# Gate and up projections of a feed-forward block by Strassen's seven products instead of eight

## The chip, the cores and the metric

One Trainium2 chip, one of its cores. The metric is the device time of one execution in microseconds (us). The kernel before has a median of 674.45 us over three runs (674.44 to 675.98).

## What is computed

One transformer block on 512 tokens of 1024 features in float32: an input norm, eight latent heads and eight sparse heads, an output projection, and a gated feed-forward part with `D_FF` = 2816. The change lies in the feed-forward part, the last lines of the reference:

```python
h = h + mixed @ w_out[l]
f = rmsnorm(h, norm_ffn_g[l])
h = h + (jax.nn.silu(f @ w_gate[l]) * (f @ w_up[l])) @ w_down[l]
return rmsnorm(h, final_norm_g)
```

## The kernel before, in words

Every float32 product is made of three products in the tensor engine's narrower `fp32r` format. Each operand is split into a rounded high part and the exact rest, and `mm3` (L167 to 170) issues high times high (L168), one part's rest times the other's high part (L169, L170), all three summing in one bank of PSUM:

```python
def mm3(o, lh, ll, rh, rl, start, stop):
    pe.matmul(o, lh, rh, start=start, stop=False)
    pe.matmul(o, lh, rl, start=False, stop=False)
    pe.matmul(o, ll, rh, start=False, stop=stop)
```

The first operand is stationary (128 x 128, loaded by an LDWEIGHTS that the profile counts under PEld), the second streams through as 128 rows by up to 512 columns.

**Order.** Up to the first two feed-forward tiles a planner (`Plan`, L55) puts the jobs of PE, DVE, ACT and POOL into a fixed order when the program is built: it knows an estimated time for each job, the jobs it waits for, the buffers it takes and frees and a priority. Each engine then runs its own list strictly in that order. The order never changes at run time, so an instruction that waits holds up everything behind it on its engine. Loads are issued from SP in the planned order too. From the third feed-forward tile on the order before is that of the code.

**Around the change.** The second half of the output projection (L1324 to 1338) makes eight products of twelve matmuls, named `mm<-w_hi,omh` in the profile, with the token tile `t` in the outer loop and the column half `nh` in the inner one; `add_out` (L1305, DVE) adds each to the residual `h`. `norm_turned` (L307) then takes a token tile: squares on ACT or DVE (L321, L323), the root of their mean on POOL (L327 to 330), scaling on DVE (L333, `xn`), eight transposes on PE (L348, `tp<-ident,xn`), a rounded copy on ACT (L362, `fTh`) and the exact rest on DVE (L368, `fTl`). So four token tiles need 32 transposes.

**Gate and up.** 22 tiles of 128 feed-forward columns. For each, two weight units of 128 x 1024 (gate, up) come in by DMA, are rounded on ACT (L158, `w_hi`) and subtracted on DVE (L162, `w_lo`); a ring of four units runs ahead. The first two tiles are made in two halves of 256 tokens (L1365, streams of 256 columns, banks `sc` and `pv`), so that they can start before the last token tiles are turned. The other twenty use streams of 512 tokens: 2 units x 8 feature tiles x 3 = 48 matmuls a tile, into the banks `mm` and `sc` in turn. `activated` (L1389) makes `silu(gate) * up` (ACT, then DVE L1403) and splits it into `a`.

**Down.** For each of the 22 tiles the weight unit `w_down` is split and 24 matmuls of 512 columns go into eight banks that hold the whole output (4 token tiles x 2 halves). The last four tiles are taken token tile by token tile, so that each one's final norm and output run beside the next one's products.

Of the kernel before, what the change touches and what calls it, by code (L numbers as in the profile page):

```python
# [10 lines left out]
F32 = mybir.dt.float32  # L11
# [18 lines left out]
# column ranges of w_in  # L30
# [7 lines left out]
def row_bcast(ap, n):  # L38
    """A DRAM row of n numbers, read into all partitions."""
    return bass.AP(tensor=ap.tensor, offset=ap.offset, ap=[[0, P], [1, n]])  # L40


class Job:
# [4 lines left out]
    def seen(self, e):  # L48
        """when an engine can go on after it"""
        if self.lag is not None:  # L50
            return self.end + self.lag
        return self.end + Plan.LAGS.get((self.eng, e), 0 if self.eng in (e, None) else Plan.LAG)


class Plan:  # L55
    """Puts jobs into the order in which their engines come to them: a job is a piece of one engine's work with
    its estimated time, the jobs it waits for, the buffers it takes and leaves, and its priority."""
# [9 lines left out]
    def add(self, ways, fn=None, after=(), pri=0.0, takes=(), frees=(), lag=None):  # L67
        """ways: (engine, ns), or several of them with the function that does it there"""
# [6 lines left out]
    def pe_end(self, t, ns, busy):  # L75
        """when the tensor engine is through with ns of work at its full clock: it has half of that after an idle tick"""
# [45 lines left out]
# priorities of the projections, as places in the row of softmaxes  # L122
# [6 lines left out]
def block_kernel(ctx: ExitStack, tc: tile.TileContext, I, out):  # L129
# [25 lines left out]
    def split(hi, lo, src, scale=None, lo_eng=None):  # L155
        """hi: src (times scale) rounded to the product's width; lo: the exact rest."""
# [10 lines left out]
    def mm3(o, lh, ll, rh, rl, start, stop):  # L167
        pe.matmul(o, lh, rh, start=start, stop=False)  # L168
        pe.matmul(o, lh, rl, start=False, stop=False)  # L169
        pe.matmul(o, ll, rh, start=False, stop=stop)  # L170
# [8 lines left out]
    class Weights:  # L179
        """Units of weights (at most 4 KB a partition), in the order of their use: loaded as they are,  # L180
        then split into two parts; loads run ahead of the splits and those ahead of the products."""
# [25 lines left out]
        def get(self, u, ahead=None):  # L207
            """unit u; the slots that its predecessors leave are filled"""
# [14 lines left out]
    kpe = px.tile([96, S], F32, name="kpe")      # rotary part of the latent keys, in rows 64-95  # L223
# [9 lines left out]
    kc = kqv.tile([P, 2, 2, 32], F32R, name="kc")    # compressed keys: group, high and low  # L233
# [4 lines left out]
    # ================= projections of the normalised input =================  # L238
# [12 lines left out]
    # weights of the latent projections: two feature tiles a unit  # L251
# [18 lines left out]
    plan = Plan(mm=2, sc=2, tp=2, pv=2, raw=2, part=3, s=4, pt=0, of=1, tmp=1, sq=1, bn=2, s4=2, rr=1, q=2, raw2=2, part2=4, cn=2, xn=2)  # L270
# [24 lines left out]
    def swapped(dst, src, sn, lead):  # L295
        """dst = the halves of src exchanged, times sn."""
# [61 lines left out]
    def split_parts(parts, after, pri, frees):  # L358
        """parts: (high, low, source, scale, columns) of one bank; all its first readers come before the second ones"""
# [21 lines left out]
    def copied(dst, src, n, after, pri, psum=True, scale=None, takes=(), frees=()):  # L381
        """a copy by the engine that comes to it first"""
# [6 lines left out]
    def split_pieces(h, l, raw, n, after, pri, takes=(), frees=()):  # L389
        """a split of operands in SBUF, given as functions, on the engines that come to it first"""  # L390
# [5 lines left out]
    def weight(pl, srcs, shape, pri, raw, part, nraw, npart, after=(), pieces=2, parts=None):  # L396
        """loads a unit of weights and splits it along its first axis, piece by piece"""
# [1136 lines left out]
```

## Time and profile before

| what | value |
|---|---|
| median of three runs | 674.45 us |
| profiled execution, as the page gives it (its span) | 670.7 us |
| median above the span | 3.75 us |
| PE busy | 643.0 us (96%) |
| DVE, ACT, POOL busy | 365.8, 284.6, 157.5 us |
| first feed-forward matmul starts | 299.20 us |
| down projection starts | 542.38 us |
| last matmul starts | 661.85 us |

The page states the profiled execution by its span alone, from the first to the last instruction, so the median stands 3.75 us above it; no other time of that execution is given. Times below are counted from the start of the span. In a row of the profile, "x160" is a count, the two numbers after the bar are the busy time in us and the mean of one in ns, and "idle before" is how long the engine had stood still. Matmuls overlap in the array, so a matmul's own length (392 ns) is not its cost; the distance from one start to the next is. In a table of stretches each engine has its busy time and, in brackets, its instructions that touch the stretch; then come the granted clock of the tensor engine (1.00 is full), the DMA share and GB/s.

### The profile page before, as it was taken

Reading aid. Unit: us, or ns where it says so; the run is one execution under the profiler, and the core shown is the slowest. Engines: PE = TensorE matmul, PEld = TensorE weight load, DVE = VectorE, ACT = ScalarE, POOL = GpSimd, SP = SyncE. Lnnn points to the kernel's source line nnn. Section 1 sums busy time; section 2 is a strip of 40 time slices with the busy share of each in tenths; the row PEclk is TensorE's granted clock in tenths of the full one; section 3 lists DMA queues with packets and bytes.
Section 4 is the critical chain, followed back from the end, with each engine's and each line's share of the span. In section 5 each row is a group of like instructions: output and inputs, shape, how many; then the busy total and the mean of one; then the engine's idle time right before and its main releaser. Section 6 shows DMA issues by size and latency. Waiting matters only on the chain.

```text
span 670.7 us, 9389 instructions
## 1 busy us (share of the span) xinstructions
PE 643.0 (96%) x3311; PEld 539.9 (80%) x3311; DVE 365.8 (55%) x867; ACT 284.6 (42%) x646; POOL 157.5 (23%) x234
## 2 busy tenths in 40 slices
PE   5899899999999999999999999999999999999994
PEld 3877698888987788789888888888888888888883
DVE  5956777898999988783343333333242422222234
ACT  4532236888997985233232222323232322221123
POOL 4621345347774742550000000000000000000013
PEclk9999889998999999999999999999999999999998
DMA  8437530121004211432232324242424243222202
GB/s 269 128 53 136 151 94 1 33 79 33 1 5 167 94 55 64 125 95 64 64 106 83 112 77 125 65 125 64 126 64 125 68 153 125 95 94 95 94 32 94
DMA packets 79424, 60.91 MB, mean 91 GB/s; under 512 B 9152, under 2 KB 71024, under 8 KB 79378
## 3 DMA queue, kind: packets, MB, share of 16 engines
q1 hardware_dynamic: 79024, 59.57, 30.5%
q8 instruction: 26, 0.43, 0.3%
q10 hardware_dynamic: 290, 0.53, 0.2%
q0 software_dynamic: 64, 0.22, 0.1%
q14 instruction: 20, 0.16, 0.1%
HBM read 57.52 MB, written 2.78 MB: 90 GB/s over the span
## 4 chain that ended last, share of the span: by engine, by line
PE 75%; DVE 10%; issue 4%; DMA 4%; POOL 3%; ACT 2%; SPq 0%; POOLq 0%; DVEq 0%; ACTq 0%
PE mm L168 11%; PE mm L169 10%; PE mm L170 10%; PE sc L169 7%; PE sc L168 7%; PE sc L170 7%; PE pv L879 3%; PE tp L845 3%; DMA ldr<-brow 2%; PE sc L1185 2%; PE pv L170 2%; PE pv L169 2%; PE pv L168 2%; DVE ptl L853 2%; PE tp L170 1%
## 5 line engine op out<-in xcount | busy, mean ns | idle before, releaser
L162 DVE TENSOR_TENSOR w_lo<-w_raw,w_hi 128x1024 fp32r<-128x1024 f32 x62 | 74.0, 1223 | 79.1 <-ACT w_hi L158 79.1
L158 ACT ACTIVATE w_hi<-w_raw 128x1024 fp32r<-128x1024 f32 x62 | 63.0, 1049 | 76.6 <-PE sc L170 71.5
L1403 DVE TENSOR_TENSOR sg<-sg,sc 128x512 f32<-128x512 f32 x21 | 14.4, 688 | 135.0 <-PE sc L170 135.0
L1462 POOL TENSOR_SCALAR ss<-ss 128x1 f32<-128x1 f32 x4 | 2.7, 684 | 351.6 <-ACT xn L1458 351.6
L158 ACT ACTIVATE a<-sg 128x512 fp32r<-128x512 f32 x22 | 13.9, 632 | 118.6 <-DVE sg L1403 118.6
L169 PE MATMUL mm<-fTl,w_hi 128*128 128x512 f32 x160 | 63.0, 394 | 0.0
L169 PE MATMUL sc<-fTl,w_hi 128*128 128x512 f32 x160 | 63.0, 394 | 0.0
L168 PE MATMUL mm<-fTh,w_hi 128*128 128x512 f32 x160 | 62.7, 392 | 0.0
L168 PE MATMUL sc<-fTh,w_hi 128*128 128x512 f32 x160 | 62.7, 392 | 0.0
L170 PE MATMUL mm<-fTh,w_lo 128*128 128x512 f32 x160 | 62.1, 388 | 0.0
L170 PE MATMUL sc<-fTh,w_lo 128*128 128x512 f32 x160 | 62.1, 388 | 0.0
L834 ACT ACTIVATE s<-s,m 128x128 f32<-128x128 f32 (+3 forms) x96 | 53.6, 560 | 12.0 <-DVE m L829 10.9
L840 POOL TENSOR_SCALAR s<-s,l,gates 128x128 f32<-128x128 f32 (+3 forms) x64 | 40.0, 629 | 31.6 <-DVE l L837 23.8
L853 DVE TENSOR_TENSOR ptl<-tp,pth 128x128 fp32r<-128x128 f32 (+3 forms) x96 | 45.0, 483 | 4.1 <-ACT pth L850 3.2
L845 PE MATMUL tp<-ident,s 128*128 128x128 f32 x240 | 42.1, 282 | 2.9 <-POOL s L840 1.1
L850 ACT ACTIVATE pth<-tp 128x128 fp32r<-128x128 f32 (+3 forms) x96 | 40.1, 433 | 7.5 <-PE tp L845 6.4
L394 POOL TENSOR_TENSOR w_lo<-w_raw,w_hi 128x512 fp32r<-128x512 f32 x25 | 33.6, 1350 | 36.6 <-DVE w_hi L391 21.1
L845 PEld LDWEIGHTS tp<-ident,s 128*128 128x128 f32 x240 | 28.4, 143 | 10.9 <-POOL s L840 5.2
L168 PEld LDWEIGHTS sc<-fTh,w_hi 128*128 128x128 f32 x160 | 30.0, 188 | 7.0
L168 PEld LDWEIGHTS mm<-fTh,w_hi 128*128 128x128 f32 x160 | 30.0, 188 | 7.0
L170 PEld LDWEIGHTS mm<-fTh,w_lo 128*128 128x128 f32 x160 | 30.0, 188 | 6.7
L170 PEld LDWEIGHTS sc<-fTh,w_lo 128*128 128x128 f32 x160 | 30.0, 188 | 6.7
(326 smaller groups left out, 1653.0 us busy)
## 6 DMA issues: line engine op xcount, KB each, us to landing
w_raw<-in_w_gate_dram SPq DMA_DIRECT2D x22, 512.0 KB, 3.9
w_raw<-in_w_up_dram SPq DMA_DIRECT2D x22, 512.0 KB, 4.9
w_raw<-in_w_down_dram SPq DMA_DIRECT2D x22, 512.0 KB, 3.4
w_raw<-in_w_in_dram SPq DMA_DIRECT2D x8, 512.0 KB, 3.8
w_raw<-in_w_out_dram SPq DMA_DIRECT2D x8, 512.0 KB, 3.7
bn<-ldr SPq DMA_DIRECT2D x16, 128.0 KB, 3.6
h<-in_x_dram SPq DMA_DIRECT2D x4, 512.0 KB, 6.5
out_dram<-xn SPq DMA_DIRECT2D x7, 256.0 KB, 2.2
```

The lines of the kernel that those rows point to most:

```text
L158: se.activation(hi, src, AF.Copy)
L162: ve.tensor_tensor(lo, src, f(hi), op=OP.subtract)
L168: pe.matmul(o, lh, rh, start=start, stop=False)
L169: pe.matmul(o, lh, rl, start=False, stop=False)
L170: pe.matmul(o, ll, rh, start=False, stop=stop)
L394: ("pool", t_pool(n), lambda: gp.tensor_tensor(l(), raw(), f(h()), op=OP.subtract))], None, [j], pri, frees=frees)
L834: se.activation(c["s"][:, 0:n], c["s"][:, 0:n], AF.Exp, bias=c["m"], scale=-1.0, accum_out=c["l"])
L840: eng.tensor_scalar(c["s"][:, 0:n], c["s"][:, 0:n], c["l"], gate(), op0=OP.mult, op1=OP.mult)
L845: pe.transpose(c["tp"][:, j * P:(j + 1) * P], c["s"][:, j * P:(j + 1) * P], ident)
L850: se.activation(c["dh"], c["src"], AF.Copy)
L853: ve.tensor_tensor(c["dl"], c["src"], f(c["dh"]), op=OP.subtract)
L879: pe.matmul(self.o[:, cs], lhs, rhs, start=self.left == self.total, stop=self.left == 1)
```

## The change

The tokens (two halves of 256), the 1024 features (two halves), and the pair gate and up make a 2 x 2 by 2 x 2 block product. Before, it takes eight block products; now it takes seven (Winograd's form of Strassen's scheme), for **two feed-forward tiles a step**, eleven steps. With A the normed tokens and B the weights (B11, B21 gate; B12, B22 up), a step makes P1 = A11 B11, P2 = A12 B21, and P6, P5, P7, P3, P4 from sums: S1 to S4 of blocks of A on the left, and on the right four sums of raw weights a step.

- **A product** is 2 column tiles x 4 feature tiles x 3 = 24 matmuls that stream 256 tokens each. A step has 168 of them, all eleven have 1848.
- **Left sums.** `ff_norm` scales the token tiles 2 and 3 by the negative root, so that sums of transposes give the wanted differences. `turned` lets PE transposes of several blocks add up in one PSUM bank: S3 is x21 + x11, then x22 is added on top for S2, then x12 for S4; A22 and S1 likewise. After each of these the bank is read (ACT `fh`, DVE `fl`) before the next transposes add to it. 64 transposes in all, and 14 reads of 512 columns.
- **Right sums** are four DVE operations of 1024 columns a step, in place in the raw tiles (L1372, L1373); each of the seven right factors is then rounded on ACT (L1553) and subtracted on DVE (L1373, `w_unit`). None of it goes to POOL.
- **Results.** P1, P6, P7 and P4 go into one bank `sc` one after the other; ACT copies it in between (L1611), so that P6 must wait for the copy of P1's state, P7 for that of P6's, and P4 for DVE's addition of it after P7 (L1621, `p<-p,sc`). P2 goes into `pv` (L1618), P5 and P3 into `mm` (L1623). Two multiplications (L1637) make `a`, unsplit; its split moves into the down stage.
- **Out projection:** `nh` becomes the outer loop, `t` the inner one, so token tile 0 is complete after the fifth product of eight and tile 3 after the last.
- **Order:** the whole rest, to the last output, is now put in order by the planner. The order of all engines up to the second half of the output projection is as before.
- The raw weights come as 128 x 4 x 256 units, four a step; eight raw tiles hold two steps. Step q+2's loads wait for the last split of step q.

The diff, cut to its core:

```diff
     h_added = []
-    for t in range(NT):
-        for nh in range(2):
+    for nh in range(2):
+        for t in range(NT):
...
-    f_ready = [norm_turned(lambda: late["fp"], lambda t=t: late["h"][:, t, :], lambda e: late["g2"][:, 512 * e:512 * e + 512], 303.5 + 4 * t, h_added[2 * t:2 * t + 2],
...
-    for ff in range(FIRST, NF):
-        res[ff] = [bank("mm"), bank("sc")]
-        for o, (wh, wl) in zip(res[ff], us):
-            for k in range(KT):
-                mm3(o, wh[:, k], wl[:, k], fTh[:, k, :], fTl[:, k, :], k == 0, k == KT - 1)
-        activated(ff - 1, res[ff - 1])
-        us = [wf.get(2 * (ff + 1 - FIRST) + c, 0) for c in range(2)]
...
+        def turned(c, q, srcs, after, pri, bk=None, tag="tp", last=True):
...
+                for n, src in enumerate(srcs):
+                    for k in range(4):
+                        pe.matmul(d["o"][:, k * P:(k + 1) * P], src()[:, k * P:(k + 1) * P], ident, is_transpose=True, start=not begun and n == k == 0,
+                                  stop=n == len(srcs) - 1, skip_group_check=True)
...
+        for q in range(2):
+            pri = 311.5 + 4 * q
+            x11, x12, x21, x22 = [lambda t=t, e=e: xn[t][e] for t in (q, q + 2) for e in range(2)]
+            d, j = turned(S3, q, [x21, x11], [x_scaled[q][0], x_scaled[q + 2][0]] + mm_free, pri, tag="mm", last=False)
+            d, j = turned(S2, q, [x22], [j, x_scaled[q + 2][1]], pri + 0.2, d, "mm", False)
+            turned(S4, q, [x12], [j, x_scaled[q][1]], pri + 0.4, d, "mm")
+            d, j = turned(A22, q, [x22], [x_scaled[q + 2][1]], pri + 0.1, last=False)
+            turned(S1, q, [x21], [j, x_scaled[q + 2][0]], pri + 0.1, d)
...
+        order_of = [(0, "P1"), (0, "P2"), (1, "P1"), (1, "P2")] + [(q, v) for q in range(NP) for v in ("P1", "P2", "P6", "P5", "P7", "P3", "P4")
+                                                                      if q > 1 or v not in ("P1", "P2")]
...
+            elif v == "P6":
...
+                need = [both(b, R[3], R[0], None, n, [r, made[1], ld[3]], pri + 2)]
...
+            elif v == "P7":
+                t1(q)
+                b = R[2]
+                need = [both(R[2], R[3], R[2], OP.subtract, n, [made[1], ld[3]], pri + 3)]
...
+            j = add(("act", t_act(n, True)), lambda: se.copy(w["p"][0], b()), [rw] + need, pri + 5)
+            j = both(lambda: w["p"][1], b, lambda: f(w["p"][0]), OP.subtract, n, [j], pri + 5)
...
+                s["made"][1] = both(R[0], R[0], R[2], OP.subtract, 1024, [s["split"]["P1"], ld[2]], s["pri"] + 1)
...
+        LEFT = {"P1": A11, "P2": A12, "P6": S2, "P5": S1, "P7": S3, "P3": S4, "P4": A22}
...
+                for n in range(2):
+                    for k in range(4):
+                        wh, wl = [x[:, k, n * P:(n + 1) * P] for x in w["p"]]
+                        mm3(d[o][:, n * HS:(n + 1) * HS], wh, wl, late["fh"][:, c, k], late["fl"][:, c, k], first and n == k == 0, k == 3, skip_group_check=True)
+
+            need = [js] + f_ready[LEFT[v]] + ([p_last] if p_last else [])
+            need += [T[q, x] for x in {"P6": ["c1"], "P7": ["u2"], "P3": ["p5"], "P4": ["c22"]}.get(v, [])]
+            p_last = add(("pe", 2832), product, need, pri + 6, takes=[BANK[o]] if first else (), frees=["part2"])
...
```

The first place is **PE's list at the end of the output projection**. Before (`fTh`, `fTl`: the normed tokens turned and split; `pth`, `ptl`: weights split into the softmaxes' old buffers):

```order
L168 MATMUL mm<-w_hi,omh 128x512
L169 MATMUL mm<-w_lo,omh 128x512
L170 MATMUL mm<-w_hi,oml 128x512
L348 MATMUL tp<-ident,xn 128x128 x8
L168 MATMUL sc<-fTh,pth 128x256
L169 MATMUL sc<-fTl,pth 128x256
L170 MATMUL sc<-fTh,ptl 128x256
```

Now (`xns`, `xnp`: scaled halves of token tiles 0 and 1, and 2 and 3; `fh`, `fl`: left factors; `w_unit`: a split right factor):

```order
L168 MATMUL mm<-w_hi,omh 128x512
L169 MATMUL mm<-w_lo,omh 128x512
L170 MATMUL mm<-w_hi,oml 128x512
L1432 MATMUL tp<-ident,xns 128x128 x8
L1432 MATMUL mm<-ident,xnp 128x128 x4
L1432 MATMUL mm<-ident,xns 128x128 x4
L1432 MATMUL tp<-ident,xnp 128x128 x4
L168 MATMUL sc<-fh,w_unit 128x256
L169 MATMUL sc<-fl,w_unit 128x256
L170 MATMUL sc<-fh,w_unit 128x256
```

Before, 24 of the 32 transposes stand between the output products or right behind them and the other 8 among the first feed-forward matmuls; now 8 stand between the output products, 20 behind the last one and 36 among the first four feed-forward products.

The second place is **DVE's list around the last output products**. Before:

```order
L1305 SCALAR_TENSOR_TENSOR h<-mm,r_74,h 128x512
L333 SCALAR_TENSOR_TENSOR xn<-h,xr,g_3831 128x512 x2
L368 TENSOR_TENSOR fTl<-tp,fTh 128x4x128
L1305 SCALAR_TENSOR_TENSOR h<-mm,r_74,h 128x512
L368 TENSOR_TENSOR fTl<-tp,fTh 128x4x128
L391 CAST w_hi<-w_raw 128x512 x2
L393 TENSOR_TENSOR w_lo<-w_raw,w_hi 128x512
L1305 SCALAR_TENSOR_TENSOR h<-mm,r_74,h 128x512
L333 SCALAR_TENSOR_TENSOR xn<-h,xr,g_3831 128x512 x2
```

Now, from the residual of token tile 1's second half on:

```order
L1305 SCALAR_TENSOR_TENSOR h<-mm,r_74,h 128x512
L1411 SCALAR_TENSOR_TENSOR xns<-h,xr,g_3823 128x512 x2
L1305 SCALAR_TENSOR_TENSOR h<-mm,r_74,h 128x512
L1372 SCALAR_TENSOR_TENSOR t_3938<-b_raw_3828,b_first 128x1024
L368 TENSOR_TENSOR fl<-tp,fh 128x4x128 x2
L1411 SCALAR_TENSOR_TENSOR xns<-h,xr,g_3823 128x512
L1305 SCALAR_TENSOR_TENSOR h<-mm,r_74,h 128x512
L1411 SCALAR_TENSOR_TENSOR xns<-h,xr,g_3823 128x512
L1411 SCALAR_TENSOR_TENSOR xnp<-h,xr,g_3823 128x512 x2
L368 TENSOR_TENSOR fl<-tp,fh 128x4x128 x2
```

The sums of weights and the scaling of tile 2 have moved in between tile 1's residual and its last subtraction, on which the first product waits.

The third place is **DVE's list in a step of gate and up**. Before, one of the first feed-forward tiles:

```order
L333 SCALAR_TENSOR_TENSOR xn<-h,xr,g_3831 128x512 x2
L368 TENSOR_TENSOR fTl<-tp,fTh 128x4x128 x2
L162 TENSOR_TENSOR w_lo<-w_raw,w_hi 128x1024 x2
L1403 TENSOR_TENSOR sg<-sg,sc 128x512
L162 TENSOR_TENSOR a<-sg,a 128x512
```

Now, from P2's result of one step to P4's of the same step (the raw tiles `b_...` of two steps in turn):

```order
L1618 TENSOR_TENSOR c_4624<-c_4624,pv 128x512
L1373 TENSOR_TENSOR w_unit<-b_raw_3828,w_unit 128x1024
L1373 TENSOR_TENSOR w_unit<-b_first,w_unit 128x1024
L1373 TENSOR_TENSOR w_unit<-b_raw_3829,w_unit 128x1024
L1373 TENSOR_TENSOR b_raw_3829<-b_raw_3829,b_late_4015 128x1024
L1621 TENSOR_TENSOR p_4716<-p_4716,sc 128x512
L1372 SCALAR_TENSOR_TENSOR t_4753<-b_late_4016,b_raw_3829 128x1024
L1373 TENSOR_TENSOR b_late_4015<-b_late_4016,b_late_4015 128x1024
L1623 TENSOR_TENSOR u_4686<-u_4686,mm 128x512
L1373 TENSOR_TENSOR w_unit<-b_raw_3830,w_unit 128x1024
L1637 TENSOR_TENSOR a<-c_4624,u_4686 128x256 x2
L1637 TENSOR_TENSOR a<-sg,p_4716 128x256 x2
```

Where a tile took one product and three subtractions, a step of two tiles now interleaves sums, splits and results, and the addition that P4 waits for (L1621) stands behind the splits of P3, P4 and the next step's P1.

More of the change, by code (lines that the diff above doesn't have):

```diff
@@ L410, in room @@
             w["h"], w["l"] = parts() if parts else [pl().tile([P] + list(shape), F32R, name=nm, tag=nm, bufs=npart) for nm in ("w_hi", "w_lo")]
[L412 to L413 removed]
+        j = w["load"] = add(("dma", n * P * 4 / 360.0), start, after, pri + PRI["wload"], takes=[raw], lag=950)
+        j = w["room"] = add((None, 0), room, [j], pri + PRI["wsplit"], takes=[part])
         return w, [split_pieces(lambda c=c: w["h"][:, piece(c)], lambda c=c: w["l"][:, piece(c)], lambda c=c: w["raw"][:, piece(c)], n // pieces,
@@ L1341, in block_kernel @@
-    fs_ctx = ExitStack()
-    FIRST = 2
-    def open_fp():
-        left_ctx.close()
-        fp = late["fp"] = pool("fp", side="left", stack=fs_ctx)
-        late["g2"] = fp.tile([P, D], F32, name="g2")
-        sy.dma_start(late["g2"], row_bcast(I["norm_ffn_g"], D))
-        late["fTh"] = fp.tile([P, KT, S], F32R, name="fTh")
-        late["fTl"] = fp.tile([P, KT, S], F32R, name="fTl")
-    fp_open = add(("dma", 1456), open_fp, [r1_ready] + [j for t in range(NT) for j in h_half[t]], 290, lag=950)
@@ L1353, in block_kernel @@
-    f_used = []
-    f_ready = [norm_turned(lambda: late["fp"], lambda t=t: late["h"][:, t, :], lambda e: late["g2"][:, 512 * e:512 * e + 512], 303.5 + 4 * t, h_added[2 * t:2 * t + 2],
-                           [fp_open] * 2, lambda: late["fTh"], lambda: late["fTl"], slice(t * P, (t + 1) * P), f_used,
-                           lambda: late["fp"].tile([P, D], F32, name="xn", tag="xn", bufs=2), after=[fp_open]) for t in range(NT)]
-    first = {}
-    for ff in range(FIRST):
-        for c, wv in enumerate((wgv, wuv)):
-            kw = dict(part="pt", parts=lambda: [a.rearrange("p j h t -> p (j h) t") for a in pair()]) if 2 * ff + c < 3 else {}
-            first[ff, c] = weight_late([(whole, wv[:, :, ff * P:(ff + 1) * P])], (KT, P), 306 + 2 * ff + c, **kw)
@@ L1379, in block_kernel @@
-    plan.run()
-    h, fp, wr, fTh, fTl = (late[k] for k in ("h", "fp", "wr", "fTh", "fTl"))
-    om_ctx.close()
-    late_aT = pool("aT", side="right")
-    NS = NF - 4
-    wf = Weights(wr, 2, 4, [((KT, P), [(whole, wv[:, :, ff * P:(ff + 1) * P])]) for ff in range(FIRST, NF) for wv in (wgv, wuv)]
-                 + [((D,), [(whole, wdv[:, ff, :])]) for ff in range(NF)])
-    aT = []
-    def activated(ff, res):
-        if ff < 6:
-            a = pa.tile([P, 2, S], F32R, name="a", tag=("pth", "ptl")[ff % 2], bufs=3)
-            aT.append((a[:, 0], a[:, 1]))
-        elif ff < 8:
-            aT.append([pa.tile([P, S], F32R, name="a", tag="s", bufs=4) for _ in range(2)])
-        elif ff < 9:
-            aT.append([pa.tile([P, S], F32R, name="a", tag=tag) for tag in ("of", "tmp")])
-        else:
-            a = late_aT.tile([P, 2, S], F32R, name=f"a{ff}")
-            aT.append((a[:, 0], a[:, 1]))
-        sg = fp.tile([P, S], F32, name="sg", tag="sg", bufs=2)
-        se.activation(sg, res[0], AF.Silu)
-        ve.tensor_tensor(sg, sg, res[1], op=OP.mult)
-        split(*aT[ff], sg)
```

389 lines of the change are left out of this document (310 added, 79 removed).

## The prediction

> **What bounds the kernel now.** I read the page's first part first, then the busy time by stretches, then the groups, then single rows in order of time. PE is busy nearly all the span:
>
> ```profile
> span 670.7 us, 9389 instructions
> PE 643.0 (96%) x3311; PEld 539.9 (80%) x3311; DVE 365.8 (55%) x867; ACT 284.6 (42%) x646; POOL 157.5 (23%) x234
> ```
>
> The stretches are the last output products, the first two feed-forward tiles (256 columns; first whole, then the part after the last transposes), the other twenty (512), the down projection, and the end:
>
> ```profile
> 272.80:298.10 25.30, 23.96 (x113) 19.04 (x111) 21.45 (x30) 8.60 (x19) 15.99 (x18) 1.00 0.41 125
> 298.10:322.65 24.55, 24.51 (x209) 24.28 (x209) 9.59 (x14) 7.40 (x10) 0.81 (x2) 1.00 0.23 65
> 304.28:322.65 18.37, 18.37 (x158) 18.37 (x157) 4.81 (x6) 5.45 (x7) 0.00 (x0) 1.00 0.21 59
> 322.65:542.38 219.73, 219.73 (x962) 180.30 (x961) 74.85 (x80) 62.57 (x80) 0.00 (x0) 1.00 0.34 96
> 542.38:662.20 119.82, 119.82 (x529) 98.91 (x527) 35.55 (x38) 28.15 (x36) 5.75 (x9) 1.00 0.28 93
> 662.20:670.70 8.50, 0.04 (x1) 0.00 (x0) 2.81 (x7) 2.35 (x7) 1.96 (x4) 0.63 0.32 123
> ```
>
> In gate and up PE never stands still at the full clock, and DVE, ACT and the DMA engines have room. Time there is matmuls times their distance. Two instructions of each count began before the stretch, so the distance is 219.73 / 960 = 0.2289 us at 512 columns and 18.37 / 156 = 0.1178 us at 256. Half the columns cost 51.5% of the time. That is the price on which the change stands.
>
> **Gate and up on PE.** Removed: 192 matmuls of 256 columns and 960 of 512, 192 x 0.1178 + 219.73 = 242.3 us. Added: 1848 of 256 columns x 0.1178 = 217.7 us. The term is -24.6 us. A seventh block product less would be -12.5%; the cost per column takes a part back. Can the distance differ for the new operands? The same form ran faster for a moment:
>
> ```profile
> 299.75 0.28 PE L169 MATMUL sc<-fTl,pth 128*128 128x256 f32 x1
> ...
> 302.58 0.28 PE L170 MATMUL sc<-fTh,ptl 128*128 128x256 f32 x1
> ```
>
> 25 distances take 2.83 us, 0.1132 each. By that the stage would be 8.5 us shorter; on the other side I allow as much above (0.1224, +8.5 us). I take 0.1178, from more than six times as many. [...]
>
> **Transposes and the start.** A group of four transposes takes 0.44 us in the chain that ended last:
>
> ```profile
> 302.86 0.44 PE tp L348 x4
> ```
>
> There are 32 more: 8 x 0.44 = 3.5 us of PE work that nothing hides. How late the first product starts hangs on the norm of token tile 1. Its chain in the trace, from the residual to the second subtraction:
>
> ```profile
> 286.85 0.73 DVE L1305 SCALAR_TENSOR_TENSOR h<-mm,r,h 128x512 f32<-128x512 f32 x1
> ...
> 287.62 0.64 ACT L321 ACTIVATE xn<-h 128x512 f32<-128x512 f32 x1 [0.61 <-DVE h L1305]
> ...
> 289.49 0.55 POOL L330 TENSOR_TENSOR xr<-ss,mhalf 128x1 f32<-128x1 f32 x1
> ...
> 290.07 1.41 DVE L333 SCALAR_TENSOR_TENSOR xn<-h,xr,g 128x512 f32<-128x512 f32 x2 [0.16 <-POOL xr L330]
> ...
> 291.64 0.60 ACT L362 ACTIVATE fTh<-tp 128x512 fp32r<-128x512 f32 x1 [0.89 <-PE tp L348]
> ...
> 293.54 0.68 DVE L368 TENSOR_TENSOR fTl<-tp,fTh 128x512 fp32r<-128x512 f32 x1
> ```
>
> That is 7.4 us (286.85 to 294.22). Now two products (24 x 0.227 = 5.4 us, 0.227 being 119.82 / 528) and 8 transposes (0.9) follow tile 1's last product, 6.3 us of cover; so the first product comes at least 1.1 us after the last output product, plus what DVE does in between by the order shown: the scaling of tiles 0 and 2 (2 x 1.41), two residuals, one sum of 1024, two subtractions for tile 0. These are some 6.7 us, of which about 3 fit into the chain's waits for ACT and POOL. I put the first product 5.0 us after the last output product. That product ends about 3.1 us earlier than the 298.1 of before (16 transposes fewer up to there, 1.8 us, and without the 1.3 us that PE was idle, 25.30 - 23.96): 295.0 + 5.0 = 300.0. Before it was 299.20:
>
> ```profile
> 298.16 1.29 PE L348 MATMUL tp<-ident,xn 128*128 128x128 f32 x8
> 299.20 0.36 PE L168 MATMUL sc<-fTh,pth 128*128 128x256 f32 x1
> ```
>
> From there 36 transposes (3.9 us) stand among the first four products, where before there were 8 (0.9). They alternate with reads: S3 is turned, read by ACT (0.60) and DVE (0.68), turned on for S2, read, turned on for S4; the products P1 and P2 of two steps, 4 x 2.83 us, lie between. Following DVE's list with the rows' durations I find it late by 1.4 us in sum at S2 and S1 of the second token tile pair. Bounds of that wait: 0 if all reads hide, 6 us if four of the reads (0.60 + 0.68 + some 0.2) stand free. The 5.0 us have 1.1 and 7.8 (nothing of the 6.7 fits) as bounds.
>
> **DVE, ACT and loads in a step.** PE needs 168 x 0.1178 = 19.8 us. The rows for the others:
>
> ```profile
> L1000 DVE TENSOR_TENSOR of<-pv,tmp 64x256 f32<-64x256 f32 x16 | 6.6, 412 | 0.2
> ...
> 402.17 2.36 DVE L162 TENSOR_TENSOR w_lo<-w_raw,w_hi 128x1024 fp32r<-128x1024 f32 x2 [0.26 <-ACT w_hi L158]
> ...
> 401.09 1.99 ACT L158 ACTIVATE w_hi<-w_raw 128x1024 fp32r<-128x1024 f32 x2
> ...
> L1403 DVE TENSOR_TENSOR sg<-sg,sc 128x512 f32<-128x512 f32 x21 | 14.4, 688 | 135.0 <-PE sc L170 135.0
> ...
> L1402 ACT ACTIVATE sg<-mm 128x512 f32<-128x512 f32 x20 | 12.0, 598 | 44.6 <-PE mm L170 44.6
> ```
>
> DVE: seven subtractions and four sums x 1.18 (half of 2.36), three additions from PSUM x 0.69, four multiplications x 0.41: 13.0 + 2.1 + 1.6 = 16.7 us, 84% of PE's step. ACT: 7 x 1.00 + 5 x 0.60 = 10.0 us. So both hide, but DVE has 3 us a step to spare where before it had far more (74.85 us of 219.73), and POOL takes none of it. The tight place is the addition (L1621) between P7 and P4: P3 gives it 2.83 us of cover, and it takes 0.69; a subtraction or sum that has just begun ahead of it takes up to 1.18, and the signals to and from DVE some 0.4. That leaves 0.6 us. Behind a waiting P4 stand the next step's P1 and P2 and so all of PE; ACT's `silu` and the multiplications wait for P4 in turn. The same holds for P6 and P7 with ACT's copies (0.60 within 2.83 us). I charge 1 us over all eleven steps, which the 0.6 us to spare would make 0; if P4 came 0.5 us late in each, it would be 5.5 us. The loads are as many bytes, 2 MB per 19.8 instead of 22 us, 106 instead of 96 GB/s, with two steps of raw tiles: nothing. On SP the second step's last two units lie where the output projection's operands were and wait for its last product, with the third step's loads behind them; those are needed two steps, some 30 us, later.
>
> **Down and end.** Both keep their matmuls: 119.82 and 8.50 us. The split of `a` (ACT 0.6, DVE 0.7 a tile) comes to 22 x 5.4 us of PE work, where DVE was busy 35.55 of 119.82 us. It hides; uncovered, DVE's part would be 22 x 0.7 = 15 us. I take 0, with 1 us for either end.
>
> **Sum.** Before: 299.20 + 0.9 + 242.3 = 542.4, as the trace has it. After: 300.0 + 3.9 + 1.4 + 217.7 + 1.0 = 524.0. The difference is -18.4 us. The profiled execution's span goes from 670.7 to 652.3; the median of the runs stands 3.75 above the span, which I leave as it is: 674.45 - 18.4 = 656.05, say 656.0 us.
>
> **The rivals.**
>
> *The clock drops at the start.* PE does 20 transposes (2.2 us) in the 5 us between the last output product and the first feed-forward one. The trace has such a gap, and what came after it:
>
> ```profile
> 84.10:87.50 3.40, 2.70 (x25) 2.62 (x25) 3.27 (x5) 0.76 (x3) 1.27 (x1) 1.00 0.55 152
> 87.50:90.90 3.40, 3.40 (x19) 3.40 (x18) 3.13 (x15) 1.84 (x5) 1.16 (x2) 0.52 0.58 159
> ```
>
> A stretch of 3.4 us with short work was followed by one at half the clock. It would cost 1.7 us, or 3.4 if two follow: 658 to 660 us. Against it: the granted clock is 1.00 from 272.8 to 662.2, through the 1.3 us of idle. [...]
>
> *DVE's order is too tight.* L1621 or the splits come late by 0.5 us a step, 5.5 us or more: 660 to 666 us. For it: 84% and a strict order; against: a ring of four split units, some 8 us of work ahead.
>
> *The faster distance.* 0.1132 us in all products: 648 us. For it: the two rows above; against: 156 matmuls at 0.1178.
>
> *Weight loads become the bound (slower).* Each matmul has a load of its own, and 256 columns leave half the time for it: PEld is busy 18.37 of 18.37 us at 256 columns, 180.30 of 219.73 at 512. A load lasts 188 ns:
>
> ```profile
> L170 PEld LDWEIGHTS sc<-fTh,w_lo 128*128 128x128 f32 x160 | 30.0, 188 | 6.7
> ```
>
> Were loads unable to overlap each other, the stage would take 1848 x 0.188 = 347 us, +130: 787 us. It decides at a distance of 0.1178 + 18.4 / 1848 = 0.128. Against it: the very stretch with PEld full ran at 0.1178. [...]
>
> *No gain.* The saved 18 us go into waits at P6, P7, P3 and P4, four a step, 0.4 us each: 674 us.
>
> **How the numbers follow.** My forecast (654 to 658) has 0.44, the clock 0.20, the tight order 0.17, the faster distance 0.09, the weight loads 0.06, no gain 0.04. The range 649 to 665 leaves out the last two, most of the faster distance and the end of the tight order, about 2 in 10. 0.3% is 2 us, about what a measurement of this kernel tells from no change: faster 0.90, the same 0.04, slower 0.06.
>
> **What would show it.** Right: seven products in 19.8 us, matmul starts 0.118 us apart; gate and up ending near 524; DVE about 16 to 17 us busy a step; PE without idle at L168 for `sc` behind L1621; first product near 300. Wrong: idle PE rows at P4 released by `p`, at P6 and P7 by ACT's copies (L1611), a granted clock under 1.00 around 300 us, or starts more than 0.128 us apart.

## The result, and the profile after

| | before | after |
|---|---|---|
| time, median of the runs | 674.45 us (672.89 to 675.98) | 657.08 us (654.24 to 659.67) |
| ratio, 95% interval | | 0.9741 (0.9708 to 0.9775) |
| span of the profiled execution | 670.7 us | 652.5 us |
| its own time | | 654.24 us |

The forecast was 656.0 us, within 649 to 665. The head of the page of after:

```profile
span 652.5 us, 11083 instructions
...
PE 624.4 (96%) x4039; PEld 556.2 (85%) x4039; DVE 472.6 (72%) x997; ACT 342.8 (53%) x724; POOL 149.6 (23%) x230
```

The busy time of after by stretches: the last output products; the gap ahead of the first feed-forward product; the first products with their transposes; gate and up; and the down projection, from its first matmul's start to its last one's. The columns are the stretch and its length, the busy time and the number of instructions of PE, PEld, DVE, ACT and POOL, the granted clock, the DMA share and GB/s.

```profile
272.80:295.00 22.20, 22.20 (x104) 18.37 (x103) 16.14 (x20) 9.42 (x20) 6.93 (x12) 1.00 0.52 166
295.00:300.00 5.00, 3.87 (x28) 2.83 (x27) 5.00 (x9) 3.98 (x8) 2.35 (x4) 1.00 0.61 194
300.00:317.00 17.00, 16.25 (x141) 16.05 (x140) 15.83 (x21) 11.45 (x18) 0.00 (x0) 1.00 0.22 67
317.00:520.00 203.00, 203.00 (x1726) 203.00 (x1725) 164.71 (x188) 103.98 (x128) 0.00 (x0) 1.00 0.38 115
522.05:645.02 122.97, 122.97 (x530) 99.08 (x528) 45.13 (x55) 36.13 (x54) 6.48 (x10) 1.00 0.19 62
```

In gate and up PE never stands still, at the full clock, and the distance is 203.00 / 1724 = 0.1177 us. DVE is busy 81% of the time. The rows that bound the stages, of after in order of time:

```profile
299.41 0.36 PE L168 MATMUL sc<-fh,w_unit 128*128 128x256 f32 x1
...
522.05 0.40 PE L168 MATMUL tp<-w_unit,fh 128*128 128x512 f32 x1
...
645.02 0.40 PE L170 MATMUL sc<-w_unit,fh 128*128 128x512 f32 x1
```

and the same boundaries of before that the prediction did not show:

```profile
542.38 0.39 PE L168 MATMUL tp<-w_hi,a 128*128 128x512 f32 x1
...
661.85 0.39 PE L170 MATMUL sc<-w_hi,a 128*128 128x512 f32 x1
```

From these the 18.2 us between the spans divide as follows. The first feed-forward product starts 0.2 us later (299.20, now 299.41). Gate and up with their transposes take 222.64 us instead of 243.18, 20.5 less. The down projection takes 122.97 us instead of 119.47, **3.5 us more**, with the same 528 matmuls. What follows the last matmul's start takes 7.5 us instead of 8.9. All that PE waited for from 285 to 645 us is two rows:

```profile
PE tp L1432 <- DVE xns L1411: 1.0, 2, 0.7
PE tp L1432 <- DVE fl L368: 0.9, 2, 0.7
```

So two things had to be tested: that the gain is the seventh product's and hangs on DVE's room, and what made an untouched stage slower. The second led to a better version.

### The profile page after: what moved, and what is told of

The parts are those of the page before. It is cut to its first block, busy times and chain, and to the rows that moved or that the text cites. A ratio compares the mean times of both kernels' runs of the same rounds, so it can differ in the third digit from the quotient of the medians.

```text
span 652.5 us, 11083 instructions
## 1 busy us (share of the span) xinstructions
PE 624.4 (96%) x4039; PEld 556.2 (85%) x4039; DVE 472.6 (72%) x997; ACT 342.8 (53%) x724; POOL 149.6 (23%) x230
## 4 chain that ended last, share of the span: by engine, by line
PE 77%; DVE 12%; DMA 4%; ACT 2%; issue 2%; POOL 1%; SPq 1%; POOLq 0%; DVEq 0%
PE mm L168 9%; PE mm L169 9%; PE mm L170 9%; PE sc L170 8%; PE sc L169 8%; PE sc L168 8%; PE pv L879 3%; PE pv L170 3%; PE pv L169 3%; PE pv L168 3%; PE tp L845 3%; DMA ldr<-brow 2%; PE sc L1185 2%; DVE ptl L853 2%; PE tp L170 2%
## 5 line engine op out<-in xcount | busy, mean ns | idle before, releaser
L170 PE MATMUL sc<-fh,w_unit 128*128 128x256 f32 x352 | 98.5, 280 | 0.0
L168 PE MATMUL sc<-fh,w_unit 128*128 128x256 f32 x352 | 98.5, 280 | 0.0
L169 PE MATMUL sc<-fl,w_unit 128*128 128x256 f32 x352 | 98.2, 279 | 0.0
L1373 DVE TENSOR_TENSOR w_unit<-b_raw,w_unit 128x1024 fp32r<-128x1024 f32 x42 | 51.3, 1222 | 48.0 <-ACT w_unit L1667 31.2
L1373 DVE TENSOR_TENSOR w_unit<-b_first,w_unit 128x1024 fp32r<-128x1024 f32 x30 | 36.7, 1222 | 43.1 <-ACT w_unit L1667 22.8
L169 PEld LDWEIGHTS sc<-fl,w_unit 128*128 128x128 f32 x352 | 66.2, 188 | 0.0
L170 PEld LDWEIGHTS sc<-fh,w_unit 128*128 128x128 f32 x352 | 66.1, 188 | 0.0
L168 PEld LDWEIGHTS sc<-fh,w_unit 128*128 128x128 f32 x352 | 65.8, 187 | 0.0
L170 PE MATMUL mm<-fh,w_unit 128*128 128x256 f32 x176 | 49.3, 280 | 0.0
L168 PE MATMUL mm<-fh,w_unit 128*128 128x256 f32 x176 | 49.1, 279 | 0.0
L169 PE MATMUL mm<-fl,w_unit 128*128 128x256 f32 x176 | 49.1, 279 | 0.0
L1553 ACT CAST w_unit<-b_raw 128x1024 fp32r<-128x1024 f32 x32 | 33.6, 1051 | 12.4 <-issue 6.0
L169 PEld LDWEIGHTS mm<-fl,w_unit 128*128 128x128 f32 x176 | 33.1, 188 | 0.0
```

Source lines behind the costliest of these rows:

```text
L168: pe.matmul(o, lh, rh, start=start, stop=False, **kw)
L169: pe.matmul(o, lh, rl, start=False, stop=False, **kw)
L170: pe.matmul(o, ll, rh, start=False, stop=stop, **kw)
L1373: return add(("dve", t_dve(n)), lambda: ve.tensor_tensor(dst(), a(), b(), op=op), after, pri, **kw)
L1553: j = add(("act", t_act(n, True)), lambda: se.copy(w["p"][0], b()), [rw] + need, pri + 5)
```

## The experiments

### The plain form in the new plan

Gate and up by four right factors and 512 columns, with the new plan, loads, tiles and end of the kernel:

```diff
-        order_of = [(0, "P1"), (0, "P2"), (1, "P1"), (1, "P2")] + [(q, v) for q in range(NP) for v in ("P1", "P2", "P6", ...
+        order_of = [(0, c, 0) for c in range(4)] + [(0, c, 1) for c in range(4)] + [(q, c, 2) for q in range(1, NP) for c in range(4)]
...
                 for n in range(2):
                     for k in range(4):
...
-                        mm3(d[o][:, n * HS:(n + 1) * HS], wh, wl, late["fh"][:, c, k], late["fl"][:, c, k], ...
+                        kk = 4 * (c % 2) + k
+                        mm3(d[g][n][:, cols], wh, wl, FT("fh")[:, kk, cols], FT("fl")[:, kk, cols], ...
```

> Gate and up in the plain form (four right factors a step, 96 matmuls of 512 columns, the first step's in two halves of 256; no sums, no negated tiles, 32 transposes), all else as in the changed kernel. Theory (the gain is the seventh block product, less the price per column): the first product at 299.3 us, 0.9 us of transposes among the first products, 192 x 0.1178 + 960 x 0.2289 = 242.3 us, so the stage ends at 542.5 instead of 521.9: 677.7 us, or 674 if the down projection goes back to 0.2267 us a matmul. Rival (the gain lies in the new order of the plan, the loads or the end): 657 to 665 us.

Measured: 676.91 us, a ratio of 1.0009 (0.999 to 1.0028) to before. Gate and up, and the down projection, of this kernel:

```profile
330.00:530.00 200.00, 200.00 (x875) 164.10 (x875) 57.63 (x55) 48.64 (x55) 0.00 (x0) 1.00 0.33 95
550.00:650.00 100.00, 100.00 (x430) 80.58 (x429) 32.27 (x35) 27.73 (x35) 0.00 (x0) 1.00 0.18 58
```

The distance is 200 / 873 = 0.2291 us in gate and up. Without the seven products the whole gain is gone, so it is theirs; the rest of the rewrite gives nothing in sum. And the down projection is slow here too (100 / 428 = 0.2336): what slowed it is not the Strassen form but something that the two kernels share.

### More work for DVE

Some of the seven split subtractions of a step are done twice: two in one kernel (P5, P3), four in the other (P1, P5, P7, P3).

```diff
             j = both(lambda: w["p"][1], b, lambda: f(w["p"][0]), OP.subtract, n, [j], pri + 5)
+            if v in ('P5', 'P3'):
+                j = both(lambda: w["p"][1], b, lambda: f(w["p"][0]), OP.subtract, n, [j], pri + 5)
```

> Two of the seven split subtractions of a step are done twice (the same values), 2 x 1.18 = 2.4 us more of DVE a step: 16.1 + 2.4 = 18.4 of PE's 19.8 us. Theory (DVE costs nothing while its sum is below PE's step): 657 us and no idle PE in the stage. Rival (DVE's order is tight, the addition between P7 and P4 has 0.6 us to spare): P4 comes late by 0.5 us or more a step, 663 us or more.

> Four of the seven split subtractions of a step are done twice, 4.7 us more of DVE a step: 20.8 us against PE's 19.8. Theory (the sum of a step decides): DVE is the bound, 1.0 us a step, ten or eleven steps: 667 to 669 us, DVE busy all through the stage. Rival (the subtractions' order has so much play that nothing is lost, or each chain is bound by itself): 657 us, or over 675 us.

Measured: 655.91 us with two (ratio to before 0.9712, 0.9679 to 0.9745), 664.86 us with four (0.9851, 0.9816 to 0.9885). Gate and up with two and then with four, and the one row of what PE waited for there with four; with two there is none:

```profile
317.00:520.00 203.00, 203.00 (x1726) 203.00 (x1725) 188.72 (x211) 103.81 (x129) 0.00 (x0) 1.00 0.40 117
```

```profile
317.00:530.00 213.00, 207.03 (x1730) 204.60 (x1729) 211.26 (x230) 103.17 (x130) 0.00 (x0) 0.99 0.36 109
```

```profile
PE mm L170 <- DVE w_unit L1373: 5.9, 11, 1.8
```

With DVE at 93% of the stretch nothing is lost; at 99% PE waits once a step. Between these two kernels the sum of a step decides, as the theory had it, and the point lies near PE's 19.8 us. The size was off: 667 to 669 us was expected, from 1.0 us a step, and the eleven waits come to 5.9 us, 0.5 a step. Some 1.7 us more (an estimate, 3.41 x 0.49) are the clock's: behind the longest wait, at 336.94, PE had half of it for a while; the ten shorter waits were followed by no such stretch.

```profile
337.87:341.28 3.41, 3.41 (x19) 3.41 (x18) 3.41 (x4) 0.07 (x1) 0.00 (x0) 0.51 0.72 173
```

The room of 0.6 us at L1621, on which the prediction put a chance of 0.17, did not matter even with 2.4 us more a step.

### Two subtractions on POOL

```diff
+            if v in ("P5", "P2") and q > 1:
+                j = add(("pool", t_pool(n)), lambda: gp.tensor_tensor(w["p"][1], b(), f(w["p"][0]), op=OP.subtract), [j], pri + 5)
+            else:
                 j = both(lambda: w["p"][1], b, lambda: f(w["p"][0]), OP.subtract, n, [j], pri + 5)
```

> From the third step on POOL makes the low parts of two right factors (P2 and P5), 2 x 2.6 us by its 512-column rows of 1352 ns, and DVE two subtractions fewer (16.1 - 2.4 = 13.7 us a step). Theory (neither engine is on the path): 657 us as before the edit. Rival (POOL and DVE hold each other up, so that DVE's rows of 1.18 us get longer; DVE's step may pass 19.8): idle PE at P4, 660 us or more.

Measured: 664.04 us, ratio to before 0.984 (0.9815 to 0.9865): DVE has two subtractions less a step, and the kernel is some 7 us slower than after. The multiplications of L1640 (L1637 in after) and one of the sums of weights (L1372), from 340 to 520 us, in this kernel and then in after, with count, busy time and mean ns:

```profile
L1640 DVE TENSOR_TENSOR a<-c,u 128x256 f32<-128x256 f32 x18 | 26.8, 1525 | 0.0
...
L1372 DVE SCALAR_TENSOR_TENSOR t<-b_raw,b_first 128x1024 f32<-128x1024 f32 x5 | 14.3, 2854 | 0.0
```

```profile
L1637 DVE TENSOR_TENSOR a<-c,u 128x256 f32<-128x256 f32 x18 | 6.8, 418 | 0.0
...
L1372 DVE SCALAR_TENSOR_TENSOR t<-b_raw,b_first 128x1024 f32<-128x1024 f32 x5 | 6.1, 1218 | 0.0
```

One such place in this kernel's rows by time, DVE first, then POOL:

```profile
382.89 0.69 DVE L1624 TENSOR_TENSOR p<-p,sc 128x512 f32<-128x512 f32 x1
383.49 2.86 DVE L1372 SCALAR_TENSOR_TENSOR t<-b_raw,b_first 128x1024 f32<-128x1024 f32 x1
```

```profile
382.86 2.41 POOL L1555 TENSOR_TENSOR w_unit<-b_first,w_unit 128x1024 fp32r<-128x1024 f32 x1 [12.14 <-ACT w_unit L1553]
```

POOL's row ends at 385.27. DVE's sum of two tiles in SBUF began at 383.49, and lasts 2.86 us, nearly the 1.78 us to POOL's end and its own 1.2 together. The addition at 382.89, one of whose inputs is in PSUM, lay beside the same POOL row and took its usual 0.69. So in these rows DVE was held, not slowed, and only with both inputs in SBUF; the additions with an input in PSUM kept means of 675 to 681 ns from 340 to 520 us (679 to 681 in after). PE waited for DVE's splits in nine steps, each time at P6. The row of the waits, and the stretch as above:

```profile
PE sc L170 <- DVE w_unit L1373: 7.1, 9, 1.3
```

```profile
317.00:525.00 208.00, 200.95 (x1694) 199.12 (x1694) 176.02 (x166) 100.86 (x126) 44.18 (x18) 1.00 0.35 108
```

DVE was busy 85% of this stretch, less than the 93% with two more subtractions, at which PE did not wait. So room in the sum of a step is not enough: the sum and the multiplications that POOL held, some 3.9 us a step longer than in after, stand in DVE's list right ahead of P6's split, and that split came late. Against this division of the work, leaving POOL out of the stage is worth those 7 us.

### The order of the output products

```diff
-    for nh in range(2):
-        for t in range(NT):
+    for t in range(NT):
+        for nh in range(2):
```

> The second half's output products come token tile by token tile again, as before the change (both column halves of tile 0, then of tile 1), not column half by column half. Theory (the order of the products is what gives the norms of tiles 0 and 1 their cover): four products instead of two follow tile 1's last one, so tiles 0 and 1 are ready in time, but tile 3's and 2's norms come as late as before; PE's waits before 317 us (1.1 and 0.75 us) go from 1.9 to 1 us: 656 us. Rival (DVE's and ACT's lists in the plan get in each other's way as they did before the change): PE stands still between the output products for 1 us or more, 658 us.

Measured: 655.61 us, ratio to before 0.9719 (0.9675 to 0.9762), not to be told from after. PE's waits from 272 to 320 us fell from 1.9 to 1.1 us, as expected:

```profile
PE mm L1432 <- DVE xnp L1411: 0.6, 1, 0.6
PE tp L1432 <- DVE fl L368: 0.5, 2, 0.3
```

An effect below 1 us is too small for these runs; whether the order helps the time stays open.

### Where the operands lie

In before, the built program puts the split activations (the stationary operand of the down projection) 480 bytes past a multiple of 512 within a partition, just where the right factors' and the down weights' units begin. After the change they lie in the left factors' tiles, which begin at 288. First both tiles were moved by 192 bytes, to 480:

```diff
+            fp.tile([P, 48], F32, name="space")
             late["fh"] = fp.tile([P, 7, 4, HS], F32R, name="fh")
```

> 192 bytes a partition are left free ahead of the left factors' tiles, which the down projection uses again for the split activations; nothing else differs. They then begin at 480 instead of 288 bytes past a multiple of 512, as the right factors' units do. Theory A (where the two operands lie decides the distance: in the kernel before it was 0.2267 us where both began at 480, and 0.2289 where one began at 288): the down projection goes from 0.2333 to 0.2267 us a matmul, 3.5 us less, 653.6 us; the 256-column products might go from 0.1178 to 0.1133, 8.2 us less again. Theory B (the place doesn't matter): 0.2333 and 0.1178 as they are, 657 us.

Measured: 655.82 us, ratio to before 0.9704 (0.968 to 0.9728). The total hides two effects of opposite sign. Gate and up, and down, of this kernel:

```profile
322.00:520.00 198.00, 198.00 (x1653) 198.00 (x1652) 157.46 (x180) 98.57 (x122) 0.00 (x0) 1.00 0.37 110
528.00:640.00 112.00, 112.00 (x496) 92.75 (x495) 40.73 (x49) 32.91 (x48) 3.86 (x7) 1.00 0.19 61
```

Down is at 112 / 494 = 0.2267 us again, 3.5 us less: the place caused the loss. Gate and up went to 198 / 1651 = 0.1199, 3.9 us more, where 0.1133 had been hoped for. So the distance changed with the place in both stages, and neither of these two places is good for both. The next kernel gives each left factor its own place:

```diff
-            late["fh"] = fp.tile([P, 7, 4, HS], F32R, name="fh")
+            late["fh"] = fp.tile([P, 7296], F32R, name="fh")
...
+        AT = {"fh": [3136, 4176, 5216, 6256, 16, 1056, 2104], "fl": [3136, 4176, 5216, 6256, 16, 1056, 2104]}
```

> Each left factor (and its low part alike) gets a place of its own: A11 begins 32 bytes past a multiple of 512, A12 96, A22 160, S1 224, S2 352, S3 416, S4 0; the right factors' units stay at 480. The splits of the activations in the down projection lie where A11, A12, S2, S1 and S3 were. The products' rows then show a distance for each place. Theory (the place within 128 bytes, against that of the other operand, decides): 96, 224 and 352 are like 480 (0.1200 in gate and up, 0.2267 in the down projection), 32, 160 and 416 like 288 (0.1178 and 0.2333), and S4's 0 is unknown. Theory (within 512 bytes): seven different distances between 0.1133 and 0.12. Rival (the distance that a stream has fallen into stays, whatever the place): one distance in all products of a step. The whole: 651 to 659 us.

Measured: 654.2 us, a single execution. One step's seven products, 24 matmuls each, in the order P1 (place 32), P2 (96), P6 (352), P5 (224), P7 (416), P3 (0), P4 (160); each stretch runs from the product's first start to the next one's:

```profile
385.66:388.49 2.83, 2.83 (x26) 2.83 (x25) 2.83 (x6) 1.54 (x2) 0.00 (x0) 1.00 0.00 0
388.49:391.33 2.84, 2.84 (x26) 2.84 (x25) 2.84 (x4) 1.54 (x2) 0.00 (x0) 1.00 0.01 3
391.33:394.18 2.85, 2.85 (x27) 2.85 (x25) 2.54 (x3) 1.69 (x2) 0.00 (x0) 1.00 0.66 187
394.18:397.04 2.86, 2.86 (x26) 2.86 (x25) 1.10 (x1) 1.53 (x2) 0.00 (x0) 1.00 0.98 315
397.04:399.78 2.74, 2.74 (x26) 2.74 (x25) 1.09 (x2) 1.54 (x2) 0.00 (x0) 1.00 0.56 177
399.78:402.59 2.81, 2.81 (x27) 2.81 (x26) 2.77 (x4) 1.05 (x1) 0.00 (x0) 1.00 0.21 69
402.59:405.31 2.72, 2.72 (x26) 2.72 (x25) 2.72 (x4) 1.05 (x1) 0.00 (x0) 1.00 0.00 0
```

The times came back alike in every step, whatever DVE and the DMA engines did beside them. Behind the first few matmuls of a product the distance is 0.1178 us at place 32 (as at 288 in after), 0.119 at 96 and 352, 0.1200 at 224 (as at 480), 0.117 at 0, and 0.1133 at 160 and 416. Equal distances went with equal places modulo 256 here, not 128 as the first theory had it. In the down projection the five places gave 0.2331 (32), 0.2325 (96), 0.2330 (352), 0.2289 (416) and 0.2266 (224). The rival, a distance that stays whatever the place, falls for these streams. In the down projection the distance went with the place in every profiled execution; in gate and up that is not the whole story, as the next kernels show.

### The places chosen

Left factors at 160 modulo 256, the split activations at 224; in a second kernel also the output products tile by tile; in a third, with the output products in the order of after, S4 alone at 0 (the second pair of lines; the numbers are the columns of 4 bytes at which the seven factors begin):

```diff
+        AT = {"fh": [96, 1120, 6240, 3168, 2144, 4192, 5216], "fl": [0, 1024, 6144, 3072, 2048, 4096, 5120]}
+        A_AT = [48, 1072, 6192, 3120, 2096, 4144, 5168]
...
-        AT = {"fh": [96, 1120, 6240, 3168, 2144, 4192, 5216], "fl": [0, 1024, 6144, 3072, 2048, 4096, 5120]}
+        AT = {"fh": [96, 1120, 6304, 3168, 2144, 4192, 5240], "fl": [0, 1024, 6208, 3072, 2048, 4096, 5144]}
```

> All left factors begin 160 bytes past a multiple of 256 (where the kernel with seven places ran at 0.1133 us a matmul, against units at 224), and the split activations of the down projection at 224 (0.2267 there). Theory (the place of the one operand against that of the other sets the distance): 1848 x 0.1133 = 209.4 instead of 217.7 us and 528 x 0.2267 = 119.7 instead of 123.2 us, 11.8 us less: 645.3 us; DVE's 16.1 us a step still fit into 168 x 0.1133 = 19.0. Rival 1 (the short distance was lent by the slower products around it): 0.1178 stays, 653.6 us. Rival 2 (the shorter products take the 0.6 us to spare at P4): the distance falls but PE waits, 650 us.

> The same places, and the output products token tile by token tile. PE's waits before 317 us were 1.1 instead of 1.9 us with that order: 644.5 us if that stays, 645.3 if not; both within what the runs can tell apart.

> As the kernel with the best places, but S4, the left factor of the sixth of a step's seven products, begins at 0 past a multiple of 256 (0.1168 in the kernel with seven places), the others at 160. The kernel with the best places had runs of 642 to 646 us and one of 653, and with the other order of the output products one of 642 and five of 649 to 652. Theory (at one place a stream of products has two patterns, 0.1133 and 0.1178; it falls into one of them after a stop and stays; products at another place push it out, and behind them it fell into 0.1133 in every step): P4 and all after it run at 0.1133 in every execution, P3 at 0.1168, 11 x 24 x 0.0035 = 0.9 us more: 643 to 647 us in every run. Rival (chance per execution): runs of 650 us and more again.

Measured: 644.02 us with the best places (median of five), ratio to before 0.9541 (0.951 to 0.9572); 649.84 us with the other order too, 0.9618 (0.9577 to 0.9659); 645.13 us with S4 apart (median of five; 645.92 with the sixth execution, of which more below), 0.9547 (0.9519 to 0.9575). Gate and up of the three kernels, in this order:

```profile
318.00:500.00 182.00, 182.00 (x1608) 182.00 (x1607) 152.11 (x174) 95.03 (x115) 0.00 (x0) 1.00 0.37 113
```

```profile
318.00:500.00 182.00, 182.00 (x1548) 182.00 (x1547) 148.39 (x168) 90.98 (x110) 0.00 (x0) 1.00 0.38 116
```

```profile
318.00:500.00 182.00, 182.00 (x1600) 182.00 (x1599) 151.20 (x174) 93.43 (x113) 0.00 (x0) 1.00 0.37 113
```

That is 182 / 1606 = 0.1133, 182 / 1546 = 0.1177 and 182 / 1598 = 0.1139 us. In the first kernel's profiled execution all of the forecast came: 8.2 us in gate and up, 3.5 in the down projection, and no new wait at P4 (PE waits for nothing in these 182 us). The second has its operands in the very same places and runs at the old distance. Its long stream began in another way after PE's last stop; each fence has the first rows behind it, of the first and of the second kernel:

```profile
315.52 0.37 PE L168 MATMUL sc<-fh,w_unit 128*128 128x256 f32 x1
315.72 0.28 PE L169 MATMUL sc<-fl,w_unit 128*128 128x256 f32 x1
315.84 0.28 PE L170 MATMUL sc<-fh,w_unit 128*128 128x256 f32 x1
315.96 0.28 PE L168 MATMUL sc<-fh,w_unit 128*128 128x256 f32 x1
316.07 0.28 PE L169 MATMUL sc<-fl,w_unit 128*128 128x256 f32 x1
```

```profile
314.33 0.37 PE L168 MATMUL sc<-fh,w_unit 128*128 128x256 f32 x1
314.53 0.28 PE L169 MATMUL sc<-fl,w_unit 128*128 128x256 f32 x1
314.81 0.38 PE L170 MATMUL sc<-fh,w_unit 128*128 128x256 f32 x1
315.03 0.28 PE L168 MATMUL sc<-fh,w_unit 128*128 128x256 f32 x1
315.15 0.28 PE L169 MATMUL sc<-fl,w_unit 128*128 128x256 f32 x1
```

The starts of the first kernel are 0.20, 0.12, 0.12 and 0.11 us apart, and from the sixth matmul on 0.113; those of the second 0.20, 0.28, 0.22 and 0.12, and then 0.118. Each stays at that for the 1750 matmuls that follow without a stop. So at one place a stream has two patterns. The gap of 0.28 us is not needed for the slower one: of the four shorter streams ahead of 315 us in the first kernel, all at place 160 and all begun with 0.20 and 0.12 or 0.11, the first ran at 0.1133 and the other three at 0.1178.

The earlier traces show that place 32 has the same two patterns. Two steps of the kernel with four subtractions done twice, in which PE stops once a step:

```profile
380.00:398.00 18.00, 18.00 (x155) 18.00 (x155) 17.96 (x21) 8.34 (x11) 0.00 (x0) 1.00 0.40 118
400.00:418.00 18.00, 18.00 (x161) 18.00 (x161) 17.96 (x21) 8.80 (x11) 0.00 (x0) 1.00 0.38 117
```

That is 18 / 153 = 0.1176 and 18 / 159 = 0.1132 us, with the same operands at the same places. Counted over all streams of 24 matmuls or more between two stops, 8 of 47 ran at 0.1133 at place 32 (in before, after, the tile order alone, both kernels with more work for DVE and the one with POOL; one more had half the clock) and 7 of 15 at place 160 (in the three kernels here); all five at 224 ran at 0.12. So between 32 and 160 the place seems to change how often a stream falls into the faster pattern after a stop (15 streams are few), and the 8.2 us are not a distance that 160 fixes.

The times of the runs agree: with the best places four took 642.8 to 645.8 us and one 653.2 (in the median, not in the ratio); with the other order one took 642.4 and five 649.4 to 651.9. The gaps, 6.5 to 10 us, are about the 8 us that 1848 x 0.0044 give. In which pattern the unprofiled runs were is inferred from their times.

S4 apart is meant as the remedy, after the step rows of the seven places: P3 at another place pushes the stream out once a step, and behind it P4 was at 0.1133 in every step. Five executions took 643.9 to 646.7 us; a sixth took 1561 us, from a cause that nothing here shows, and is left out of the ratio. Whether the remedy works is not shown. The kernel without it, in the same order of the output products, had four of five below 646 us as well, and the profiled execution with S4 apart ran at 0.1133 already ahead of its first P3, so no stream is seen there being pushed out of 0.1178. It costs 0.0006 us a matmul, 1.1 us. Its five executions are 12 to 13 us faster than after (by the medians and by the ratios): 645.13 against 676.17 us of before on the same chip.

### The plain form with places chosen

The plain form again, with the same places (160), and then with the moving operands at 224:

```diff
-        AT = {"fh": 96, "fl": 0}
+        AT = {"fh": 48, "fl": 80}
```

> The plain form (four right factors, 512 columns) with the same places: moving operands at 160, units at 224, the split activations at 224. Theory: the down projection at 0.2267 (-3.5 us); the 960 products of 512 columns at 0.2267 to 0.2289 (0 to -2.1 us), the 192 of 256 at 0.1133 (-0.9): 676.9 - 4.4 to 6.5 = 670.4 to 672.5 us. Then the seventh product is worth 26 us with places chosen in both forms, where it was 20 without. Rival (512 columns gain as much a column as 256 do): 0.2240 or less, 668 us.

> The plain form again, with its moving operands at 224 past a multiple of 256, where the units lie too; the split activations of the down projection are at 224 as before. Theory (both operands alike gave 0.2267 wherever 512 columns were moved; 160 gave 0.2333): 960 x 0.2267 = 217.6 instead of 219.7 us, the 192 products of 256 at 0.1200 (+0.4), the down projection -3.5: 676.9 - 5.2 = 671.7 us. Rival (the streams of 512 columns too fall into one of several patterns by chance): 0.2289 or 0.2333 as before, 673 to 678 us.

Measured: 678.21 us at 160, ratio to before 1.0042 (1.0017 to 1.0066), a miss; 673.0 us at 224, 0.9955 (0.9933 to 0.9976). Gate and up of the first and of the second:

```profile
330.00:530.00 200.00, 200.00 (x859) 161.15 (x858) 56.54 (x54) 47.55 (x54) 0.00 (x0) 1.00 0.32 93
```

```profile
330.00:530.00 200.00, 200.00 (x884) 165.64 (x884) 57.27 (x55) 48.22 (x55) 0.00 (x0) 1.00 0.33 98
```

At 160, the best place for 256 columns, 512 columns run at 200 / 857 = 0.2334 us, the slowest seen in this stage; at 224, the worst for 256, at 200 / 882 = 0.2268. So the best place here depended on the number of columns as well. With places chosen in each form the seven products are worth 673.0 - 645.1 = 28 us, as long as the seven are in the faster pattern; in the other it would be some 8 us less (an estimate, 1848 x 0.0044). With the places as they fell it was 676.9 - 657.1 = 20.

## Why the prediction was right, and where it was not

- **Pace of gate and up: right.** 0.1177 us a matmul against 0.1178, the term that carried the sum. On both forms of the kernel, all that was measured in gate and up and in the down projection lies at 0.1132 to 0.1200 us with 256 columns and 0.2266 to 0.2336 with 512.
- **Transposes and start: right, a little high.** The first product came at 299.41 (forecast 300.0). The wait set at 1.4 us at S2 and S1 was one of 0.74 at S1. The clock, on which a rival had 0.20, is 1.00 in all stretches around it.
- **DVE hidden: right.** 164.71 / 203.00 of PE's 19.8 us is 16.1 us a step (forecast 16.7). The 1.0 us charged for a tight order was nothing, and the kernel with two more subtractions shows that there was room for 2.4 us. That the order can bind while the sum has room was a sound fear all the same: with POOL's two subtractions it did, at P6 and not at L1621.
- **Gate and up's end** was 522.05, not 524.0: mainly the start, the wait and the charge just told.
- **Down and end: wrong.** The step took the down projection as unchanged within 1 us because its matmuls are the same; it took 3.5 us more. "Both keep their matmuls" missed that the operands had moved: the distance 0.2333 instead of 0.2267 goes with the place of the split activations, and came back with it. With what followed the last matmul 1.4 us shorter (not tested), this made up for the 2 us won before. That the spans differ by 18.2 us where 18.4 was forecast is luck to that extent: two errors of 2 us cancel.
- **The faster distance** had a chance of 0.09, weighed by how many matmuls had shown each distance. The short stretch of before was no accident of counting but the second pattern of the same place; in other kernels at place 32 whole steps ran in it, and at 160 a whole stage. How many matmuls had shown a distance says little where a stream keeps what it fell into. That rival was better than its weight, though after did not show it.
- **Weight loads as the bound: no.** PEld is full (182.00 of 182.00) at 0.1133 us too; a full PEld row was no sign of a limit at 0.1178.
- **From span to median:** the forecast added 3.75 us, measured were 657.08 - 652.5 = 4.6. The profiled execution's own time is only 1.74 above its span; the rest is that it was the fastest of four.

## What to carry to other kernels

Compare the distance of like matmuls, stage by stage, before and after a change, in stages too that the change leaves alone: a per cent or three there may come only from where the tiles now lie, and here 192 bytes of space brought it back in the down projection (0.2333 to 0.2267 us). Where a stream can have two patterns, one profile of each kernel does not tell the effect of a place; count the streams and look at every run. When an engine off the path gets more work, add up its time over one step against the step of the bounding engine and test the tipping point by doing work twice. The sum is a condition, not a guarantee: with DVE at 93% nothing was lost, and at 85% PE waited in each of the nine steps with work on POOL, because the work that got longer stood right ahead of a split that PE needs. Work given to an idle POOL was not free for DVE here: beside a POOL subtraction its sum of two SBUF tiles took 2.86 us instead of 1.22.

## What the runs showed of the hardware that was not expected

- The distance of matmuls that waited for nothing went with the places of stationary and moving operand within a partition, modulo 256 bytes: 0.1133 to 0.1200 us at 256 columns, 0.2266 to 0.2336 at 512, with the other operand's units at 224. The units themselves were never moved. Why the places should matter, no run shows.
- At 256 columns a stream had one of two patterns (0.1133 and 0.1178 us) at one and the same place, at 32 as at 160; it fell into one after a stop and kept it for 1750 matmuls. The place seems to change how often (the faster one in 8 of 47 streams at 32, in 7 of 15 at 160). What in the hardware makes the patterns, and what chooses at a stop, stays open: streams whose first starts lie equally far apart took either.
- After one stop of 1.8 us, in the kernel with four subtractions done twice, PE had half its clock (0.51) for 3.4 us; after ten shorter ones in the same kernel it had not.
- DVE's sum of two SBUF tiles that began beside a POOL subtraction ended only after it (2.86 instead of 1.22 us), while an addition with an input in PSUM beside the same one kept its 0.69 us.
